# A DiT block's FFN: the first product as a pipeline in a written order, with two units' weight forms made ahead and parked in DRAM

## The chip, the cores and the metric

The kernel runs on one core of one Trainium2 chip. The core has five engines that run side by side, each with its own queue: TensorE (PE, matrix products into PSUM), VectorE (DVE), ScalarE (ACT), GpSimd (POOL) and SyncE (SP, which here issues DMAs). The metric is the device time of one execution in microseconds; the lower the better. All matrix products are made of matmuls with a 128x128 stationary operand and up to 512 moving columns.

## The reference

The program is one block of a diffusion transformer: 1024 tokens of width 1024, in float32, batch 1. What matters here is its second half:

```python
x_new = layer_norm(ALPHA * x + mx[2] * (mix_x @ w_out[l]), ln1_g[l], ln1_b[l])
ffn_x = conv_ffn(modulate(x_new, mx[3], mx[4]), ffn_up[l], ffn_conv_w[l], ffn_conv_b[l], ffn_down[l], rows)
x_new = layer_norm(ALPHA * x_new + mx[5] * ffn_x, ln2_g[l], ln2_b[l])

def conv_ffn(h, w_up, conv_w, conv_b, w_down, grid_rows):
    a, g = jnp.split(h @ w_up, 2, axis=-1)
    a = dwconv3x3(a.reshape(bsz, grid_rows, t // grid_rows, f), conv_w).reshape(bsz, t, f) + conv_b
    return (jax.nn.gelu(a, approximate=False) * g) @ w_down
```

`modulate` is a layer norm over the 1024 features, then a scale and a shift. `ffn_up` is 1024 x 5632 (a half `a` and a gate half `g` of 2816 each), `ffn_down` is 2816 x 1024. The convolution is 3x3 over a grid of 16 x 64 tokens, for each feature by itself.

## The kernel before

Every product is made of three matmuls: each float32 operand is split into a high part (a cast on ACT) and a low part (a subtraction on DVE or POOL), and high x high, high x low and low x high are added in PSUM (`split`, L91; `mm3`, L112).

**w_out** (`out_proj`, L895) takes the tokens in eight row tiles of 128. For each, PE makes 48 matmuls; DVE adds the residual and does the layer norm; after row tiles 2 and 4 the two finished ones are normalised again, modulated and transposed by PE (`modulate2`, L951, `shift2`, L944), which gives the forms "11" and "21" of the FFN's input for the first four row tiles, and copies of them in DRAM (`xr`). Row tiles 4 to 7 stay in SBUF as `ly`.

**FFN, first product.** The 2816 features make 22 units of 128, each with an a column and a g column of `w_up`. A unit's product is done with seven block products instead of eight, Strassen's scheme in Winograd's form: the input X (features x tokens) is cut in four blocks, and so is the unit's weight (a11, a12 of the a column, a21, a22 of the g column). Product k takes one form of the weight and one form of the input (`FORM`, L972): 1 takes a11 and X11, 2 takes a12 and X21, 6 takes S2 and T2, 5 takes S1 and T1, 7 takes a11 - a21 and T3, 3 takes a12 - S2 and X22, 4 takes a22 and T4, with S1 = a21 + a22 and S2 = S1 - a11. One product is 12 matmuls; a unit has 84. The sums of products go through a PSUM bank `x` (tag B, four banks) and a pair `zv` (tag A, two pairs), with copies on ACT and additions on DVE (`after`, L1089).

The weight forms are made in `weight_form` (L983): sums on POOL, the high part on ACT, the low part on POOL, into one of six W tiles. The last part of a unit is the convolution: eight taps on DVE (L1117) on top of a centre tap on ACT (L1096), then the gelu (L1120), the two products with the gate (L1125) and a store of h to DRAM (`hd`, L1126).

`up_begin` (L1023) makes products 1 and 2 of units 0 and 1 and product 1 of units 2 and 3 (72 matmuls) from forms loaded beside w_out (`load_form`), then transposes the last four row tiles (`one`, L1043), makes T2, T1, X22, T3 and T4 from them (`two`, L1053), and runs products 6, 5, 3, 7, 4 of units 0 and 1 together. `ffn_up` (L1135) runs the rest one unit after the other in the order 1, 2, 6, 5, 3, 7, 4, and in units 2 to 9 also makes one column of the modulation (`ada_col`) each. All of this is given to the tile framework, whose scheduler puts each engine's instructions in an order of its own; `high_priority(AHEAD)` lets loads go ahead.

**w_down** (`ffn_down`, L1153) goes over the tokens in two groups of four row tiles, over all 22 units in each; it loads h and w_down again and splits them.

## Time and profile before

| what | us |
|---|---|
| median of three runs | 1412.34 (1410.67 to 1415.03) |
| the profiled execution | 1411.74 |
| its span, first to last instruction | 1409.9 |
| PE busy, share of the span | 1291.0 (92%) |
| DVE busy | 973.6 (69%) |
| ACT busy | 532.7 (38%) |
| POOL busy | 339.6 (24%) |

A busy PE is one that has matmuls in flight. A line such as `L1117 DVE ... x176 | 214.1, 1224 | 5.2 <-ACT` names the line of the kernel, the engine, the operation with its output and inputs, the count, the busy time in us and the mean in ns, and the idle time before it with what ended it. A timeline row starts with the time from the span's start and the duration, both in us. A row of the table by windows gives, for a stretch, each engine's busy time with its number of instructions, then the clock granted to PE (1.00 is full), the share of the DMA engines in use and GB/s.

### The profile page before, as it was taken

To read this page: it belongs to the slowest core of one execution; us is meant where nothing else is said; L and a number is where in the kernel's file an instruction comes from. 1 tells how busy PE (TensorE), PEld (TensorE's weight loads), DVE (VectorE), ACT (ScalarE), POOL (GpSimd) and SP (SyncE) were. 2 spreads that over 40 slices of the span, in tenths; PEclk is the share of its full clock that TensorE was granted. 3 is DMA by queue.
4 is the path that set the end of the run, shared out by engine and by line. 5 is a ranking of instruction groups with operands and counts; after the bars stand their busy time and mean duration, and the time that the engine had idled before them with its cause. 6 is when DMAs were issued, how large, how long until landed. Compare 5 with 4: busy or idle time off the path is not lost.

```text
span 1409.9 us, 17494 instructions
## 1 busy us (share of the span) xinstructions
PE 1291.0 (92%) x6466; PEld 1069.0 (76%) x6466; DVE 973.6 (69%) x1717; ACT 532.7 (38%) x978; POOL 339.6 (24%) x258
## 2 busy tenths in 40 slices
PE   4999999999999999996547999999999959999997
PEld 3888988898888887875435788777878748888885
DVE  7869944869587785888463967666777663339547
ACT  4744434433332413345312344444443423333330
POOL 0000000000000000022808777777777600000000
PEclk9999999999999999998677999999999989999999
DMA  9672310132131541353014422222222128446622
GB/s 336 223 241 72 119 61 30 38 113 75 60 105 31 181 131 66 120 180 134 1 42 158 143 90 75 90 76 75 90 75 90 45 98 290 136 155 215 210 91 89
DMA packets 66661, 163.97 MB, mean 116 GB/s; under 512 B 7808, under 2 KB 10512, under 8 KB 66576
## 3 DMA queue, kind: packets, MB, share of 16 engines
q1 hardware_dynamic: 66576, 162.86, 34.3%
q8 instruction: 50, 0.82, 0.2%
q14 instruction: 35, 0.29, 0.1%
HBM read 140.79 MB, written 22.04 MB: 115 GB/s over the span
## 4 chain that ended last, share of the span: by engine, by line
PE 42%; DVE 6%; POOL 2%; DMA 2%; issue 1%; ACT 1%; DVEq 0%; SPq 0%; POOLq 0%; ACTq 0%
PE psB L1019 5%; PE psB L1021 5%; PE psB L1020 5%; PE psA L1019 4%; PE psA L1020 4%; PE psA L1021 4%; PE psA L114 3%; PE psA L116 3%; PE psA L115 3%; DVE psA L1117 3%; PE psB L114 3%; PE psB L116 3%; PE psB L115 3%; POOL s L997 1%; POOL wf L95 1%
## 5 line engine op out<-in xcount | busy, mean ns | idle before, releaser
L1117 DVE SCALAR_TENSOR_TENSOR psA<-a,par,psA 128x945 f32<-128x945 f32 (+2 forms) x176 | 214.1, 1224 | 5.2 <-ACT psA L1096 1.3
L95 POOL TENSOR_TENSOR wf<-raw,wf 128x512 fp32r<-128x512 f32 x104 | 138.8, 1338 | 115.1 <-ACT wf L94 115.0
L95 POOL TENSOR_TENSOR wf<-r,wf 128x512 fp32r<-128x512 f32 x6 | 8.6, 1464 | 515.3 <-ACT wf L94 515.3
L114 PE MATMUL psA<-xh,wh 128*128 128x512 f32 x320 | 126.7, 396 | 2.3 <-ACT wh L94 1.2
L116 PE MATMUL psA<-xh,wl 128*128 128x512 f32 x320 | 126.0, 394 | 0.1
L115 PE MATMUL psA<-xl,wh 128*128 128x512 f32 x320 | 126.0, 394 | 0.0
L94 ACT CAST wf<-raw 128x512 fp32r<-128x512 f32 x104 | 64.0, 618 | 147.8 <-PE psB L1021 100.5
L95 DVE TENSOR_TENSOR dwl<-r,dwh 128x512 fp32r<-128x512 f32 x80 | 52.4, 690 | 85.5 <-ACT dwh L94 85.1
L1019 PE MATMUL psB<-xk,wf 128*128 128x512 f32 x176 | 73.9, 420 | 36.7 <-DVE r L1122 18.3
L1020 PE MATMUL psB<-x,wf 128*128 128x512 f32 x264 | 104.1, 394 | 0.0
L1095 DVE TENSOR_TENSOR a<-psA,s 128x512 f32<-128x512 f32 x44 | 30.3, 690 | 92.5 <-PE psA L1021 92.5
L94 ACT CAST dwh<-r 128x512 fp32r<-128x512 f32 x80 | 46.6, 620 | 107.8 <-PE psB L116 80.6
L1019 PE MATMUL psA<-x,wf 128*128 128x512 f32 x176 | 72.3, 412 | 8.5 <-ACT wf L94 8.5
L1021 PE MATMUL psB<-xk,wf 128*128 128x512 f32 x176 | 71.8, 408 | 6.5 <-POOL wf L95 6.5
L94 ACT CAST wh<-r 128x512 fp32r<-128x512 f32 x72 | 42.0, 618 | 86.4 <-PE psA L115 59.0
L1019 PEld LDWEIGHTS psB<-xk,wf 128*128 128x128 f32 x176 | 34.8, 198 | 52.3 <-DVE r L1122 26.1
L95 DVE TENSOR_TENSOR wl<-r,wh 128x512 fp32r<-128x512 f32 x72 | 47.5, 688 | 35.9 <-ACT wh L94 22.7
L1019 PE MATMUL psB<-x,wf 128*128 128x512 f32 x176 | 69.1, 392 | 3.0 <-ACT s L1099 3.0
L114 PEld LDWEIGHTS psA<-xh,wh 128*128 128x128 f32 x320 | 60.2, 188 | 14.4 <-ACT wh L94 1.6
L1020 PE MATMUL psA<-x,wf 128*128 128x512 f32 x176 | 69.9, 397 | 0.0
L1021 PE MATMUL psA<-x,wf 128*128 128x512 f32 x176 | 69.6, 395 | 0.2 <-POOL wf L95 0.2
L116 PEld LDWEIGHTS psA<-xh,wl 128*128 128x128 f32 x320 | 60.2, 188 | 12.3 <-DVE wl L95 0.5
(349 smaller groups left out, 3590.3 us busy)
## 6 DMA issues: line engine op xcount, KB each, us to landing
raw<-in_wup SPq DMA_DIRECT2D x44, 512.0 KB, 3.5
r<-in_w_down SPq DMA_DIRECT2D x88, 256.0 KB, 3.2
ada<-in_ada SPq DMA_DIRECT2D x32, 512.0 KB, 3.6
r<-in_win SPq DMA_DIRECT2D x56, 256.0 KB, 2.8
hd<-h SPq DMA_DIRECT2D x22, 512.0 KB, 2.6
hr<-hd SPq DMA_DIRECT2D x44, 256.0 KB, 4.2
adat<-in_ada SPq DMA_DIRECT2D x16, 512.0 KB, 6.9
cada<-in_ada SPq DMA_DIRECT2D x11, 512.0 KB, 5.1
```

The source lines that it names most:

```text
L94: nc.scalar.copy(hi, src)
L95: (on or nc.vector).tensor_tensor(out=lo, in0=src, in1=hi.bitcast(F32), op=ALU.subtract)
L114: mm(out, lh, rh, start=first, stop=False)
L115: mm(out, lh, rl, start=False, stop=False)
L116: mm(out, ll, rh, start=False, stop=last)
L997: pool.tensor_tensor(out=out, in0=x, in1=y, op=op)
L1019: mm(bank, w[:, 0, c], xh, start=start and j == 0, stop=False, skip_group_check=True)
L1020: mm(bank, w[:, 0, c], xl, start=False, stop=False, skip_group_check=True)
L1021: mm(bank, w[:, 1, c], xh, start=False, stop=j == 3, skip_group_check=True)
L1095: nc.vector.tensor_tensor(out=self.a[:, g], in0=z, in1=c, op=ALU.add)
L1117: nc.vector.scalar_tensor_tensor(out=o, in0=a3[:, r0 + di:r1 + di, c0 + dj:c1 + dj], scalar=cw(i, j), in1=o, op0=ALU.mult, op1=ALU.add)
```

## The change

It rewrites the first product of the FFN; w_out's own work and w_down's products stay.

- **Order.** All engines are wrapped (`Engine`), and while `pinned` is set each instruction keeps its place in the program on its engine. The whole of `ffn_up` is pinned. A unit's products come in the order 1, 2, 6, 5, 7, 3, 4, and `step` runs one product, then what follows it, then prepares the weight form five products ahead (`prepare`): the cast on ACT, the subtraction on POOL one step later (`low`). The gelu of a unit comes after product 6 of the next unit, the products with the gate and the store after its product 5.
- **Unit 0 plain.** Unit 0 is done without the seven products, as 96 matmuls (`up_plain`): its first half, on X11 and X21, together with products 1 and 2 of unit 1, takes 72 matmuls ahead of the transposes; its second half follows the transposed tiles three behind.
- **Parking.** The forms of unit 1 (6, 5, 7, 3, 4) and of unit 2 (all seven) are made on POOL beside w_out (`park`: four sums each, a copy and a subtraction for each form) and stored in DRAM by DMAs from POOL's queue; `prepare` loads them back.
- **T forms.** The forms 12 (for the plain unit, in the tiles of T4), 22, T2, T1 and T3 are split on ACT and DVE; T4 on ACT and POOL.
- **Ahead of w_down.** `down_first` loads w_down and h of the first three units during the last unit and splits them on ACT and POOL; w_down begins with these, row tile by row tile in the order 0, 2, 1, 3, banks B for the first two. The last two stores of h go out from POOL's queue.
- The modulation columns are made two at a time in units 5, 7, 9 and 11.

```diff
+        parks = self.park(op, 1, (6, 5, 7, 3, 4)) + self.park(op, 2, (1, 2, 6, 5, 7, 3, 4))
...
+                    if parks and kt in (order[3], order[7]):
+                        parks.pop(0)()
...
+            if t == 7:
+                self.norm2([ys[j] for j in (4, 5, 6)])
...
+    def park(self, op, u, ks):
...
+        def sums():
+            a11, a12, a21, a22 = parts()
+            s = self.Wt((2, 512), F32, nm="ws")
+            r["S1"], r["S2"] = s[:, 0], s[:, 1]
+            pool.tensor_tensor(out=r["S1"], in0=a21, in1=a22, op=ALU.add)
+            pool.tensor_tensor(out=r["S2"], in0=r["S1"], in1=a11, op=ALU.subtract)
+        def sums2():
+            a11, a12, a21, a22 = parts()
+            pool.tensor_tensor(out=a12, in0=a12, in1=r["S2"], op=ALU.subtract)
+            pool.tensor_tensor(out=a21, in0=a11, in1=a21, op=ALU.subtract)
+        def one(k):
+            a11, a12, a21, a22 = parts()
+            src = {1: a11, 2: a12, 3: a12, 4: a22, 5: r.get("S1"), 6: r.get("S2"), 7: a21}[k]
+            w = self.Wt((2, 512), nm="wp")
+            pool.tensor_copy(w[:, 0], src)
+            pool.tensor_tensor(out=w[:, 1], in0=src, in1=w[:, 0].bitcast(F32), op=ALU.subtract)
+            d = self.parked[u, k] = self.dp.tile([P, 2, 512], F32, name=self.name("wd"))
+            nc.gpsimd.dma_start(d, w.bitcast(F32))
...
+        return [raws, sums] + [one_(k) for k in early] + [sums2] + [one_(k) for k in ks if k not in early]
...
+        while self.prepared < min(n + 1, len(self.plan)):
+            u, k = self.plan[self.prepared]
+            self.prepared += 1
+            if (u, k) in self.parked:
+                self.forms[u, k] = self.Wt((2, 512), nm="wf")
+                nc.sync.dma_start(self.forms[u, k].bitcast(F32), self.parked[u, k])
+                continue
...
+            w = self.Wt((2, 512), nm="wf")
+            self.nc.scalar.copy(w[:, 0], src)
+            self.low()
+            self.pending = (w, src)
+            self.forms[u, k] = w
...
+    def low(self):
+        if self.pending:
+            w, src = self.pending
+            self.nc.gpsimd.tensor_tensor(out=w[:, 1], in0=src, in1=w[:, 0].bitcast(F32), op=ALU.subtract)
+            self.pending = None
...
+        b = self.bank("B")
+        self.product(1, b, w11, True)
+        nc.scalar.copy(u1.s[:, 0], b)
+        u0.zv, u1.zv = self.pair(), self.pair()
+        self.up_plain(u0.zv[:, 0], a0, 0)
+        self.product(2, b, w12, False)
+        nc.scalar.copy(u1.a[:, 0], b)
+        ga, gb = self.bank("B"), u1.zv[:, 0]
+        self.up_plain(ga, g0, 0)
+        for j in range(4):
+            nc.sync.dma_start(xa[j // 2][:, j % 2], self.xr[j][:, 0])
+        self.norm2(ys[3:])
...
+        def direct(kt):
+            i, j = kt // 4, kt % 4
+            self.shift2(self.bank("B"), ys, kt, v[j][:, i])
+            self.split(v[j][:, i], *self.form(("12", "22")[i], j))
...
+        order = [0, 4, 1, 5, 2, 6, 3, 7]
+        extra, lag = [], 3
+        for i in range(KT + lag):
+            if i < KT:
+                direct(order[i])
+            if i >= lag:
+                kt = order[i - lag]
+                xh, xl = self.form(("12", "22")[kt // 4], kt % 4)
+                for bank, w in ((u0.zv[:, 1], a0), (gb, g0)):
+                    self.mm3(bank, w[0][:, kt, :], w[1][:, kt, :], xh, xl, i == lag, i == KT + lag - 1)
+            if i == 2:
+                nc.scalar.copy(u0.r[:, 0], ga)
+            if i == 3:
+                self.prepare(1)
+            if i % 2 and i < KT:
+                extra += sums(i // 2)
+            for _ in range(2):
+                if extra:
+                    extra.pop(0)()
+        for f in extra:
+            f()
+        for j in range(4):
+            self.split(xa[j], *self.form("T2", j))
...
+        go(u2, 7)
+        tt(out=u2.r[:, 1], in0=u2.x, in1=u2.r[:, 0], op=ALU.add)
+        self.prepare(self.at + 5)
+        u1.conv()
+        go(u2, 3)
+        tt(out=u2.a[:, 1], in0=u2.v, in1=u2.s[:, 1], op=ALU.add)
+        u2.centre(1, u2.a[:, 1])
+        self.prepare(self.at + 5)
+        go(u1, 4)
+        self.prepare(self.at + 5)
+        u1.gelu()
+        go(u2, 4)
+        self.prepare(self.at + 5)
+        u1.finish((u1.x, u1.r[:, 1]))
+        u2.conv()
+        self.prev = u2
...
+            if k == 2:
+                r[0] = [self.Wt(nm="dwh")]
+                high(r[0][0], flat(0))
+            elif k == 6:
+                r[0].append(self.Wt(nm="dwl"))
+                low(r[0][1], r[0][0], flat(0))
...
+            elif k == 6:
+                nc.scalar.copy(self.s[:, 1], self.x)
+                if b.prev:
+                    b.prev.gelu()
...
+            (nc.sync if self.f < FT - 2 else nc.gpsimd).dma_start(b.hd[self.f], self.h.rearrange("p g t -> p (g t)"))
```

Where the change moves instructions, three places. First POOL's queue from the last instruction ahead of w_out on. Before (`wf` is a weight form, `x` and `xv` belong to the FFN's input, `r` is a raw load):

```order
L293 IOTA masktmp_1084 128x128
L95 TENSOR_TENSOR wf_5647<-r_5648,wf_5647 128x512
L95 TENSOR_TENSOR wf_5652<-r_5653,wf_5652 128x512
L95 TENSOR_TENSOR wf_5657<-r_5658,wf_5657 128x512
L95 TENSOR_TENSOR wf_5662<-r_5663,wf_5662 128x512
L95 TENSOR_TENSOR wf_5667<-r_5668,wf_5667 128x512
L95 TENSOR_TENSOR wf_5672<-r_5673,wf_5672 128x512
L95 TENSOR_TENSOR x_816_5775<-xv_5930,x_814_5773 128x512
```

and with the change (`raw` is a unit's raw weight, `ws` its sums, `wp` a parked form, `wd` its place in DRAM; all calls go through the wrapper's line 57):

```order
L57 TENSOR_TENSOR ws_4901<-raw_4887 128x512
L57 TENSOR_TENSOR ws_4901<-ws_4901,raw_4885 128x512
L57 TENSOR_TENSOR raw_4887<-raw_4885,raw_4887 128x512
L57 TENSOR_TENSOR raw_4885<-raw_4885,ws_4901 128x512
L57 CAST wp_4930<-ws_4901 128x512
L57 CAST wp_4987<-ws_4901 128x512
L57 TENSOR_TENSOR wp_4930<-ws_4901,wp_4930 128x512
L57 TENSOR_TENSOR wp_4987<-ws_4901,wp_4987 128x512
L57 DMA wd_4933<-wp_4930 128x1024
L57 DMA wd_4990<-wp_4987 128x1024
L57 CAST wp_5004<-raw_4887 128x512
```

POOL's first work beside w_out was six subtractions at its end; now 32 operations and twelve DMAs of the parked forms stand there, of which these are the first, and two of the six remain behind them.

Second, ACT's queue where the transposed last row tiles are read. Before (`psA` are the two banks of the pairs that the transposes used in turn; `t2`, `xraw`, `xv` are sums of the input's blocks, `xk` and `x2` their split forms):

```order
L949 ACTIVATE xv855_5930<-psA824_5783,mods_107 128x512
L949 ACTIVATE xv855_5930<-psA825_5784,mods_107 128x512
L949 ACTIVATE xv858_5948<-psA824_5783,mods_107 128x512
L94 CAST x2_814_5773<-xv855_5930 128x512
L94 CAST xk811_5770<-t2856_5931 128x512
L949 ACTIVATE xv858_5948<-psA825_5784,mods_107 128x512
L94 CAST xk812_5771<-xraw854_5929 128x512
```

and with the change (`r881` is the first half of unit 0's gate, out of bank `psB885`):

```order
L57 ACTIVATE xv872_5912<-psB892_6021,mods_107 128x512
L57 CAST xk860_5900<-xv872_5912 128x512
L57 ACTIVATE xv872_5912<-psB893_6029,mods_107 128x512
L57 CAST x2_862_5902<-xv872_5912 128x512
L57 ACTIVATE xv873_5913<-psB894_6039,mods_107 128x512
L57 CAST xk860_5900<-xv873_5913 128x512
L57 COPY r881_5921<-psB885_5975 128x512
L57 ACTIVATE xv873_5913<-psB895_6049,mods_107 128x512
```

The tile that comes out of a transpose is now cast at once, without a sum ahead of it, and the transposes go round four B banks, the fourth of which (`psB895`) is the one that the copy of `psB885` frees.

Third, the end of POOL's queue, in the FFN's last unit. Before:

```order
L95 TENSOR_TENSOR wf1243_9036<-raw1231_8959,wf1243_9036 128x512
L95 TENSOR_TENSOR wf1245_9064<-raw1232_8960,wf1245_9064 128x512
L95 TENSOR_TENSOR wf1246_9081<-raw1232_8960,wf1246_9081 128x512
L1285 UNCONDITIONAL_BRANCH
L1285 ISA
```

and with the change (`dw` and `dr` belong to w_down's weights, `dh` to its h, `hd` is h in DRAM):

```order
L57 TENSOR_TENSOR wf1271_9064<-raw1233_8761,wf1271_9064 128x512
L57 TENSOR_TENSOR dwl1275_9098<-dr1264_9038,dwh1273_9081 128x1024
L57 DMA hd20_95<-h1274_9096 128x1024
L57 TENSOR_TENSOR dhw1278_9120<-dr1267_9041,dhw1278_9120 128x512
L57 TENSOR_TENSOR dwv1279_9123<-dr1266_9040,dwv1279_9123 128x1024
L57 TENSOR_TENSOR dhr1281_9127<-dr1267_9041,dhr1280_9126 128x512
L57 TENSOR_TENSOR dwl1283_9167<-dr1265_9039,dwh1282_9143 128x1024
L57 TENSOR_TENSOR dhw1284_9181<-dr1268_9042,dhw1284_9181 128x512
L57 DMA hd21_96<-h1285_9184 128x1024
```

The low parts of w_down's first three units and the stores of the last two units' h have moved here.

More of the change, by code (lines that the diff above doesn't have):

```diff
@@ L44, in strided, with __init__, __getattr__, call @@
     return bass.AP(t.tensor, t.offset + off, [list(t.ap[0])] + [list(d) for d in dims])
+class Engine:
+    def __init__(self, b, engine):
+        self.b, self.engine = b, engine
+    def __getattr__(self, name):
+        f = getattr(self.engine, name)
+        def call(*args, **kw):
+            ins = f(*args, **kw)
+            return self.b.tc.keep_in_program_order(ins) if self.b.pinned else ins
+        return call
+class Engines:
+    def __init__(self, b, nc):
+        for e in ("tensor", "vector", "scalar", "gpsimd", "sync"):
+            setattr(self, e, Engine(b, getattr(nc, e)))
 class Builder:
@@ L50, in __init__ @@
     def __init__(self, tc, a, out):
-        self.tc, self.nc, self.a, self.out = tc, tc.nc, a, out
+        self.tc, self.a, self.out = tc, a, out
+        self.pinned = False
+        self.nc = Engines(self, tc.nc)
         self.n = 0
@@ L981, in load_form, with load_raws @@
         return w
[L983 to L992 removed]
+    def load_raws(self, u):
+        ra, rg = self.S((2, 512), nm="raw"), self.S((2, 512), nm="raw")
+        for r, f in ((ra, u), (rg, FT + u)):
+            self.nc.sync.dma_start(r.rearrange("p j (k f) -> p (j k) f", f=P), self.a["wup"][f])
+        self.raws[u] = dict(a=ra, g=rg)
@@ L1014, in product @@
+            self.forms[u, k] = w
+        if self.prepared == len(self.plan):
+            self.low()
+    def low(self):
[3 more added lines that the diff above has]
+            self.pending = None
+    def product(self, k, bank, w, start):
+        mm = self.nc.tensor.matmul
         for j in range(4):
@@ new lines, in product, with up_plain @@
+            mm(bank, w[:, 0, c], xh, start=start and j == 0, stop=False, skip_group_check=True)
+            mm(bank, w[:, 0, c], xl, start=False, stop=False, skip_group_check=True)
+            mm(bank, w[:, 1, c], xh, start=False, stop=j == 3, skip_group_check=True)
+    def up_plain(self, bank, w, g):
+        for kt in range(KT):
+            xh, xl = self.form(("11", "21", "12", "22")[2 * g + kt // 4], kt % 4)
+            self.mm3(bank, w[0][:, kt, :], w[1][:, kt, :], xh, xl, kt == 0, kt == KT - 1)
@@ L1128, in units @@
-    def units(self, us, ks):
-        for k in ks:
-            ws = [self.weight_form(u.f, k) for u in us]
-            self.product(k, [(u.open(k), w, k in (1, 2, 5)) for u, w in zip(us, ws)])
-            for u in us:
-                u.after(k)
-    def ffn_up(self):
-        nc = self.nc
-        bufs = dict(raw=4, a=2, s=2, r=2, h=3)
-        self.ut = lambda kind: self.up.tile([P, 2, 512], F32, tag=kind, bufs=bufs[kind], name=self.name(kind))
-        silc = self.up.tile([P, D], F32, tag="row", bufs=2, name="silc5")
-        nc.sync.dma_start(silc, self.silc[0:1].broadcast_to([P, D]))
-        for f in range(2, FT):
-            if f < 10:
-                t = self.up.tile([P, D], F32, tag="row", bufs=2, name=self.name("ada"))
-                nc.sync.dma_start(t, self.a["ada"][38 + f])
-                self.ada_col(38 + f, silc, self.mods[:, 38 + f:39 + f], [t])
-            elif f == 10:
-                self.gate5 = self.gate_line(5)
-            if f < 4:
-                self.units([self.begun[f - 2]], (2, 6, 5, 3, 7, 4))
-            else:
-                self.units([self.Unit(self, f)], (1, 2, 6, 5, 3, 7, 4))
+                tt(out=self.a[:, 1], in0=self.zv[:, 1], in1=self.s[:, 1], op=ALU.add)
@@ L1157, in ffn_down @@
             LAST = 3 if g == 0 else 7
-            banks = [[self.bank("A" if t < 2 else "B") for _ in range(2)] for t in range(4)]
-            late = []
+            order = (0, 2, 1, 3) if g == 0 else range(4)
+            banks = {t: [self.bank(("B" if t < 2 else "A") if g == 0 else "A" if t < 2 else "B") for _ in range(2)] for t in order}
+            late, early = [], []
             def work(t, c, f, hh, wh, wl):
@@ L1226, in ffn_down, with down_load @@
                     self.finish(ys[t], t, lng, lnb, st)
+    def down_load(self, dn, g, f, i):
+        nc, hh = self.nc, None
+        if i is not False:
+            if i % 2 == 0:
+                self.big = self.kp.tile([P, 4, D], F32R, tag="kq", bufs=2, name=self.name("dwk"))
+            wh, wl = self.big[:, 2 * (i % 2), :], self.big[:, 2 * (i % 2) + 1, :]
+            hh = self.Wt((2, 512), nm="dhw")
+        else:
+            wh = dn.tile([P, D], F32R, tag="dwh", bufs=4, name=self.name("dwh"))
+            wl = dn.tile([P, D], F32R, tag="dwl", bufs=4, name=self.name("dwl"))
+            hh = dn.tile([P, 2, 512], F32R, tag="dh", bufs=4, name=self.name("dh"))
+        hh = hh[:, 0, :], hh[:, 1, :]
+        for c in range(2):
+            c = slice(c * 512, (c + 1) * 512)
+            self.load_split(self.a["w_down"][f * P:(f + 1) * P, c], wh[:, c], wl[:, c])
+        with self.tc.high_priority(self.AHEAD):
+            h = dn.tile([P, 512], F32, tag="hr", bufs=6, name=self.name("hr"))
+            nc.sync.dma_start(h, self.hd[f][:, g * 512:(g + 1) * 512])
+            self.split(h, *hh)
+        return wh, wl, hh
     def load_xnew(self, dn, t):
```

377 lines of the change are left out of this document (242 added, 135 removed).

## The prediction

> **What bounds the kernel now.** I read the page's slices first, then busy times by stage, then the timelines inside the stages that stand out.
>
> ```profile
> PE   4999999999999999996547999999999959999997
> PEclk9999999999999999998677999999999989999999
> ```
>
> TensorE (PE) is full everywhere but in two dips, slices 19 to 22 and 33; its clock falls there too. The stages, by windows:
>
> ```profile
> core 0: us, PE busy (x) PEld busy (x) DVE busy (x) ACT busy (x) POOL busy (x), PEclk, DMA share, GB/s
> 552.50:609.10 56.60, 56.60 (x255) 45.38 (x254) 45.94 (x145) 20.87 (x62) 0.00 (x0) 1.00 0.25 84
> 635.30:652.30 17.00, 17.00 (x80) 14.10 (x79) 12.71 (x48) 5.69 (x10) 0.00 (x0) 1.00 0.52 189
> 652.30:809.30 157.00, 97.02 (x369) 72.93 (x367) 101.33 (x107) 55.62 (x91) 96.81 (x68) 0.78 0.25 86
> 809.30:1138.00 328.70, 328.70 (x1418) 263.47 (x1419) 228.46 (x221) 138.15 (x220) 233.07 (x177) 1.00 0.23 77
> 1138.00:1158.30 20.30, 4.85 (x21) 3.34 (x20) 12.30 (x12) 2.42 (x3) 0.00 (x0) 0.74 0.23 68
> 1158.30:1401.00 242.70, 242.25 (x1056) 198.72 (x1056) 134.40 (x245) 75.58 (x137) 0.00 (x0) 0.99 0.53 177
> 1401.00:1409.90 8.90, 0.00 (x0) 0.00 (x0) 5.62 (x13) 0.20 (x1) 0.00 (x0) 0.66 0.15 59
> ```
>
> The w_out product (to 635.3) and the FFN from 809.3 to 1138 leave PE no idle time. From 652.3 to 809.3 PE works 97 of 157 us at a clock of 0.78, and before w_down 20.3 us pass. These two are what the change can win. What fills the first, from PE's timeline and the chain of waits:
>
> ```profile
> 676.96 0.80 PE L1019 MATMUL psB<-xk,wf 128*128 128x512 f32 x1 [14.05 <-ACT s L1087]
> ```
> ```profile
> 708.38 16.02 DVE psA L1117 x15
> 736.11 6.53 DMA raw<-in_wup
> ```
>
> PE waits 14 us for the forms of the last four row tiles, then 16 us for the convolutions of two units run together, then for a weight load that stood in SP's queue behind a store.
>
> **The change, part by part.** *Steady stretch.* A unit begins here every 19.50 us, 84 matmuls at 0.232 (chain of waits):
>
> ```profile
> 828.61 0.67 PE psB L1019 x2
> 848.11 0.68 PE psB L1019 x2
> ```
> ```profile
> L1117 DVE SCALAR_TENSOR_TENSOR psA<-a,par,psA 128x945 f32<-128x945 f32 (+2 forms) x176 | 214.1, 1224 | 5.2 <-ACT psA L1096 1.3
> ```
> ```profile
> L95 POOL TENSOR_TENSOR wf<-raw,wf 128x512 fp32r<-128x512 f32 x96 | 128.4, 1341 | 106.7 <-ACT wf L94 106.7
> ```
>
> The new order keeps 84 matmuls and gives each engine's instructions in program order. I walked one unit through the queues. Per unit DVE has eight taps (9.8 us) and some 4 us of additions; the ada columns now come two at a time in four units, two more operations of 1024 columns, each like a tap: 16.3 us. POOL has eleven operations at 1.34, 14.7 us, and a form is ready four products before its use. Pinning adds one wait that others stand behind: ACT's gelu waits for the previous unit's convolution, and behind it stand a cast and the copy of product 5. That convolution starts when product 3 ends, at 16.7, and ends near 28.5, 9 us into the next unit; the copy is wanted when product 3 starts, at 14. So 19.5 stays; POOL would bind only above 19.5/11 = 1.77 us an operation.
>
> *Start of the FFN.* PE first gets 72 matmuls, as many as before, then the transposes of the last four row tiles:
>
> ```profile
> 651.63 1.03 PE L948 MATMUL psA<-ident,ly 128*128 128x128 f32 x8
> ```
> ```profile
> 655.04 0.62 ACT L94 CAST xk<-t 128x512 fp32r<-128x512 f32 x1
> 655.56 0.78 ACT L949 ACTIVATE xv<-psA,mods 128x512 f32<-128x512 f32 x1
> 656.23 0.61 ACT L94 CAST xk<-xraw 128x512 fp32r<-128x512 f32 x1
> ```
> ```profile
> 660.33 0.68 DVE L95 TENSOR_TENSOR x<-xraw,xk 128x512 fp32r<-128x512 f32 x1
> 660.93 0.68 DVE L1048 TENSOR_TENSOR xraw<-xv,xraw 128x512 f32<-128x512 f32 x1
> ```
>
> From 651.6 on these now run beside the second half of unit 0's plain products, which need no sums, only the tile split once; before, every next product needed T2. The splits that POOL made here (forms 22 and T3) go to DVE, and POOL, which holds DVE up (below), is nearly idle. A tile costs ACT 0.67 + 0.52 = 1.19 us, DVE 0.60 an operation. PE's fourth transpose needs the bank that ACT empties only after three tiles and a copy, 4.9 us in; three transposes fill 1.6, so PE idles 3.3, and I add 2 for a lowered clock. DVE's 20 operations (eight splits, twelve sums) end some 14 us in, with POOL's four subtractions between them 17, and T2's four splits at 19.4; its first use is at 24. ACT casts T1 after unit 0's end (18.7) and T3 after two copies, so T3 is done at 26.5, wanted at 31. To the end of unit 2: 32 transposes 4.1, the remaining 48 + 60 + 84 = 192 matmuls 44.5, one matmul with the identity (no row: 0.23 like a product's to four transposes' 0.52; I take 0.5, it is f32 as they are), 5.3 for the fill: 54.4, so 706.0. Parked forms come by DMA five products (14 us) ahead, and a load lands in 3.5:
>
> ```profile
> raw<-in_wup SPq DMA_DIRECT2D x44, 512.0 KB, 3.5
> ```
>
> Then DVE is late, since three convolutions come in 45 us. Unit 0's runs from 26.5 to 36.3. Unit 1's stands in DVE's queue behind the addition after unit 2's product 7, which ends at 44.9: it ends at 55, its gelu at 59, and unit 3's second product needs that pair of banks at 56: 2.7 us. Unit 2's convolution ends at 70, and its gelu stands ahead of the copy that unit 3's product 3 waits for: 2.5. Bounds: 0, if the fill is longer and hides it, to 10, one chain of eight taps. I take 5.2, by the walk: 711.2. With 19 units at 19.5 the FFN ends at 1081.7, against 1138. Before, 328.7/19.5 = 16.9 units were left at 809.3, so 5.1 were done; now 5.1 are done at 711.2 + 2.1 x 19.5 = 753.
>
> *w_out.* Here POOL had nothing before 622. Parking gives it 32 operations (20 with two inputs, twelve casts), twelve DMA issues and four loads on SP. A row for its casts does not exist: between ACT's 0.62 and POOL's 1.34. An issue on POOL: SP's 0.33 to 1.34; that is 4 to 16 us of POOL, off the path. What counts is what POOL does to DVE:
>
> ```profile
> 622.22 1.07 DVE L136 TENSOR_TENSOR nwt<-vet,rst 128x1 f32<-128x1 f32 x1
> 625.82 2.29 DVE L866 SCALAR_TENSOR_TENSOR ly<-ly,rst,ln_b 128x1024 f32<-128x1024 f32 x1
> 632.23 0.16 DVE L136 TENSOR_TENSOR nwt<-vet,rst 128x1 f32<-128x1 f32 x1
> 632.81 1.28 DVE L866 SCALAR_TENSOR_TENSOR ly<-ly,rst,ln_b 128x1024 f32<-128x1024 f32 x1
> ```
> ```profile
> 621.95 8.57 POOL L95 TENSOR_TENSOR wf<-r,wf 128x512 fp32r<-128x512 f32 x6 [515.27 <-ACT wf L94]
> ```
>
> With POOL at work a DVE operation that reads two SBUF tiles takes 1.0 us longer (1.07 for 0.16, 2.29 for 1.28). And PE has no slack for it: the normalised tile is done by ACT at 583.64, its transpose ran at 583.82, at a fixed place in PE's queue, which the change leaves where it was; behind it stand all of w_out's later matmuls. A second norm step stands 25 us later in the same way.
>
> ```profile
> 582.40 1.24 ACT L942 ACTIVATE ly<-ly,nmt,rst 128x1024 f32<-128x1024 f32 x1 [1.45 <-DVE nmt L941]
> ```
> ```profile
> 583.82 0.49 PE L948 MATMUL psB<-ident,ly 128*128 128x128 f32 x3
> ```
> ```profile
> L149 DVE BATCH_NORM_STATS2 bnst<-ly 128x6 f32<-128x512 f32 x22 | 14.1, 678 | 0.0
> L931 DVE SCALAR_TENSOR_TENSOR ly<-ly,psA 128x512 f32<-128x512 f32 x14 | 9.0, 672 | 0.0
> ```
>
> DVE is busy 45.9 of 56.6 us there; in the 10.7 it idles some eight of POOL's operations fit. The statistics and the PSUM additions, 23 us and some small ones, read one SBUF tile, and L931 at 0.67 shows no delay; the other 0.6 of DVE's busy time reads two. 24 x 0.6 x 1.0 = 14 us lost. Bounds: 0, if POOL fits into what is idle, to 32 x 1.34 = 43 (a lower clock after each of two stalls is in it). I take 14, since the two rows with POOL beside them are of this very stage. By the Trainium skill (SBUF — State Buffer, Who interferes with whom) the two engines share a port as a lock, and the later one blocks for the other's whole instruction. The trace agrees in kind, at 1.0 us where whole operations take 1.34; by the rule's letter the 14 would be 24 x 0.6 x 1.34 = 19.
>
> The new wait on SP: the raw weights of unit 2 wait until POOL is done with unit 1's, and the load of x for row tile 2 and three stores stand behind them.
>
> ```profile
> 564.55 0.33 SPq L922 DMA_DIRECT2D ly<-in_x  x1
> ```
>
> POOL can start near 552; twelve operations and two issues later it is 572. With 3.5 to land, x is there at 576; the product that it is added to ends 34 matmuls, 8 us, ahead of the transpose at 583.82, so near 576: free, or as late as POOL is, which the 43 covers.
>
> *w_down.* The chain of waits in the second dip:
>
> ```profile
> 1139.56 1.21 DVE psA L1117
> 1150.17 1.03 ACT h L1120
> 1153.00 4.53 DMA hr<-hd
> 1158.28 0.80 PE psA L114
> 1161.62 0.23 PE psA L115
> ```
>
> Convolution, gelu, product, store and reload, then eight matmuls at half speed. Now the weights and h of the first three tiles are made during the last unit by ACT and POOL, and PE goes on with 72 matmuls (16 us), longer than the last unit's 10.4 us of convolution, gelu and product. Only row tile 1's second bank waits for that product: 1.5. Without this cover the 20.3 come back. w_down takes 242.7 less 2.0 of slow start, the end 8.9.
>
> **Sum.** 1081.7 + 14 + 1.5 + 240.7 + 8.9 = 1346.8 against 1409.9, less 63. The profiled run's time was 1411.74, 1.84 over its span, and the median 1412.34 is 0.6 above that: 1346.8 + 2.4 = 1349.
>
> **Rivals.**
> 1. *Parking is free*: DVE's delay fits in gaps. For it: DVE idles 10.7 us of the 56.6. Against: 0.18 us of slack. 1349 - 14 = 1335. Chance 0.17.
> 2. *Every POOL operation blocks DVE whole*, 43 us instead of 14: 1378. For it: DVE is 0.8 full, so delays add up. Against: one-tile operations between. Chance 0.13. The lock of the Trainium skill (SBUF — State Buffer, Who interferes with whom) is this mechanism.
> 3. *The fill fails*: DVE late with T2 or T3 and a gap of one convolution pair, 16 us, with slow clock 22: 1371. For it: DVE is the fullest engine there. Chance 0.12.
> 4. *w_down's start is not covered*, the change not doing there what it says (the lows of w_down and the last two stores stand in POOL's one queue): plus 19, 1368. Chance 0.06.
> 5. *Slower*: in the pinned order every unit waits for POOL's lows. From 1.77 us an operation it decides; at 2.15 a unit takes 23.7, plus 4.2 x 19 = 80: 1429. For it, POOL beside a busy DVE:
>
> ```profile
> 671.33 1.71 POOL L997 TENSOR_TENSOR s<-raw 128x512 f32<-128x512 f32 x1
> ```
>
> Against: 1.34 in the steady stretch, beside the same DVE work per unit. Chance 0.04.
>
> **How the numbers follow.** Forecast 0.48, own range 1340 to 1359 (w_out 5 to 24). The range 1332 to 1376 takes in rivals 1, 3, 4 and part of 2 and leaves out 5. A measurement tells 0.3%, 4.2 us, from no change: faster 0.94, same 0.01, slower 0.05.
>
> **What would show it.** DVE's small operations near 1.1 us in w_out beside POOL, and PE idle before the transposes of both norm steps there; one PE gap of 3 to 5 us after the first 72 matmuls; units 19.5 apart; no PE gap over 2 us before w_down. Wrong: a steady unit above 20, w_out unchanged or more than 30 us longer, or a gap over 10 us in the first three units.

## The result, and the profile after

| | before | after |
|---|---|---|
| median of four runs, us | 1412.7 (1410.7 to 1415.0) | 1368.7 (1364.4 to 1371.5) |
| ratio, 95% interval | | 0.969 (0.966 to 0.972) |
| profiled execution: time, span | 1411.74, 1409.9 | 1371.46, 1369.7 |

The change makes the kernel 3.1% faster: 44 us, where the prediction had 63. In the profile of the change every line is that of the wrapper (L57), so groups are told by their tiles. The slices of the page after:

```profile
PE   4999999999999999949998999999999999999997
POOL 0000000000000000560027766677777740000000
PEclk9999999999999999969999999999999999999999
```

Before w_down (slice 33 before) no dip is left, and that at the start of the FFN has shrunk to one 8. A new dip stands in slice 17, inside w_out, just where POOL has got work. The stages, by windows: w_out, the first 72 matmuls of the FFN, the rest up to the end of unit 2, unit 3, units 4 to 11, units 12 to 21, w_down, end.

```profile
core 0: us, PE busy (x) PEld busy (x) DVE busy (x) ACT busy (x) POOL busy (x), PEclk, DMA share, GB/s
540.90:660.98 120.08, 99.16 (x417) 77.01 (x417) 101.90 (x228) 41.33 (x125) 41.61 (x46) 0.90 0.46 165
660.98:677.35 16.37, 16.37 (x73) 13.47 (x72) 11.47 (x40) 6.53 (x10) 0.00 (x0) 1.00 0.46 154
677.35:731.02 53.67, 50.00 (x228) 39.50 (x226) 44.79 (x52) 31.40 (x51) 19.16 (x14) 1.00 0.50 178
731.02:757.46 26.44, 21.27 (x86) 16.78 (x84) 19.83 (x20) 10.78 (x17) 16.82 (x14) 0.94 0.33 112
757.46:922.84 165.38, 156.65 (x674) 128.06 (x672) 122.49 (x129) 66.15 (x104) 113.46 (x90) 0.98 0.33 116
922.84:1113.39 190.55, 190.55 (x842) 157.68 (x841) 130.86 (x131) 84.44 (x131) 137.70 (x107) 1.00 0.24 82
1113.39:1360.10 246.71, 242.36 (x1057) 198.75 (x1055) 139.83 (x248) 73.77 (x133) 4.22 (x4) 0.99 0.51 170
1360.10:1369.70 9.60, 0.16 (x1) 0.00 (x0) 5.62 (x13) 0.20 (x1) 0.00 (x0) 0.65 0.15 55
```

Ten units in 190.55 us are 19.05 a unit, so the steady pipeline runs at PE's pace. What is lost lies in four places. The first and largest, from PE's and ACT's timelines in w_out (in brackets the idle time before, and what ended it):

```profile
600.35 0.48 PE L57 MATMUL psB<-ident,ly 128*128 128x128 f32 x1 [14.52 <-ACT ly L57]
607.20 0.90 PE L57 MATMUL psB<-ident,ly 128*128 128x128 f32 x3 [2.96 <-ACT ly L57]
```
```profile
599.05 1.24 ACT L57 ACTIVATE ly<-ly,nmt,rst 128x1024 f32<-128x1024 f32 x1 [15.10 <-DVE nmt L57]
```

PE waits 14.5 us for the first transpose of the norm step, and the norm waits for DVE. What DVE and POOL did in that time:

```profile
589.03 0.69 DVE L57 TENSOR_TENSOR ml<-O,mh 128x128 fp32r<-128x128 f32 x1
589.64 5.47 DVE L57 TENSOR_TENSOR ml<-sgo,mh 128x128 fp32r<-128x128 f32 x2
595.03 3.14 DVE L57 TENSOR_TENSOR ml<-O,mh 128x128 fp32r<-128x128 f32 x1
598.10 0.15 DVE L57 SCALAR_TENSOR_TENSOR rst<-nwt,rst 128x1 f32<-128x1 f32 x1
```
```profile
588.90 0.67 POOL L57 CAST wp<-raw 128x512 fp32r<-128x512 f32 x1
...
590.11 1.27 POOL L57 TENSOR_TENSOR wp<-raw,wp 128x512 fp32r<-128x512 f32 x1
591.34 1.26 POOL L57 TENSOR_TENSOR raw<-raw,raw 128x512 f32<-128x512 f32 x1
592.54 0.57 POOL L57 DMA_DIRECT2D wd<-wp  x1
593.13 1.27 POOL L57 TENSOR_TENSOR raw<-raw,ws 128x512 f32<-128x512 f32 x1
594.34 1.23 POOL L57 CAST wp<-ws 128x512 fp32r<-128x512 f32 x2
```

The last three of these tile splits, 0.28 us each when POOL is idle, take 8.6 us here, while POOL makes unit 2's forms. The chain's small operation `rst`, 0.15 long, stands behind them. Summed over DVE's timeline from 553 to 610 us (each operation less the shortest of its form), 19 operations are held up by 22.5 us in all, beside 32 POOL operations of 33.5 us. This sum is "DVE held up" in the table below.

The other three places: unit 3 (26.4 us for 19.04); four units of 4 to 11, those with two modulation columns, which take 21.5 to 23.1; and a stall in w_down, 20 us after its start. Rows of PE's timeline for each:

```profile
737.29 4.57 PE L57 MATMUL psA<-x,wf 128*128 128x512 f32 x12 [3.39 <-ACT h L57]
751.87 3.03 PE L57 MATMUL psA<-x,wf 128*128 128x512 f32 x12 [1.78 <-ACT psA L57]
792.44 4.60 PE L57 MATMUL psA<-x,wf 128*128 128x512 f32 x12 [2.18 <-ACT psA L57]
834.61 3.01 PE L57 MATMUL psA<-x,wf 128*128 128x512 f32 x12 [2.18 <-ACT psA L57]
1133.83 0.50 PE L57 MATMUL psB<-dwh,dh 128*128 128x512 f32 x1 [2.94 <-ACT dh L57]
```

### The profile page after: what moved, and what is told of

Its sections match the earlier page's. It is cut to its first block, busy times and chain, and to the rows that moved or that the text cites. A ratio compares the mean times of both kernels' runs of the same rounds, so it can differ in the third digit from the quotient of the medians.

```text
span 1369.7 us, 17583 instructions
## 1 busy us (share of the span) xinstructions
PE 1284.1 (94%) x6480; PEld 1074.6 (78%) x6480; DVE 977.1 (71%) x1712; ACT 528.3 (39%) x966; POOL 334.1 (24%) x279
## 5 line engine op out<-in xcount | busy, mean ns | idle before, releaser
L57 DVE SCALAR_TENSOR_TENSOR psA<-a,par,psA 128x945 f32<-128x945 f32 (+2 forms) x176 | 215.9, 1227 | 21.6 <-ACT psA L57 16.2
L57 PE MATMUL psA<-x,wf 128*128 128x512 f32 x708 | 175.7, 398 | 15.2 <-ACT psA L57 11.8
L57 PE MATMUL psB<-xk,wf 128*128 128x512 f32 x672 | 176.8, 390 | 1.0 <-ACT s L57 1.0
L57 PEld LDWEIGHTS psA<-x,wf 128*128 128x128 f32 x708 | 135.5, 192 | 46.6 <-ACT psA L57 14.3
L57 PEld LDWEIGHTS psB<-xk,wf 128*128 128x128 f32 x672 | 126.2, 188 | 27.9 <-ACT s L57 1.4
L57 POOL TENSOR_TENSOR wf<-raw,wf 128x512 fp32r<-128x512 f32 x95 | 124.5, 1322 | 62.8 <-ACT wf L57 62.7
L57 PE MATMUL psA<-xh,wh 128*128 128x512 f32 x320 | 127.4, 398 | 2.1 <-ACT wh L57 1.2
L57 PE MATMUL psA<-xh,wl 128*128 128x512 f32 x320 | 126.6, 396 | 0.1
L57 PE MATMUL psA<-xl,wh 128*128 128x512 f32 x320 | 126.6, 396 | 0.0
L57 POOL TENSOR_TENSOR ws<-raw 128x512 f32<-128x512 f32 x2 | 2.6, 1282 | 460.3 <-DMA raw<-in_wup 460.3
L57 DVE TENSOR_TENSOR dwl<-r,dwh 128x512 fp32r<-128x512 f32 x74 | 48.4, 688 | 81.1 <-ACT dwh L57 81.0
L57 PE MATMUL psB<-x,wf 128*128 128x512 f32 x384 | 104.7, 389 | 0.0
L57 PE MATMUL psB<-dwh,dh 128*128 128x512 f32 x296 | 98.5, 394 | 2.9 <-ACT dh L57 2.9
L57 PE MATMUL psA<-dwh,dh 128*128 128x512 f32 x296 | 97.3, 390 | 0.7 <-DVE fy L57 0.7
L57 PEld LDWEIGHTS psB<-x,wf 128*128 128x128 f32 x384 | 72.1, 188 | 15.4 <-issue 0.2
L57 ACT CAST dwh<-r 128x512 fp32r<-128x512 f32 x74 | 43.0, 619 | 102.8 <-PE psA L57 67.0
L57 ACT CAST wh<-r 128x512 fp32r<-128x512 f32 x76 | 44.6, 618 | 92.1 <-PE psA L57 64.5
L57 DVE TENSOR_TENSOR a<-psA,s 128x512 f32<-128x512 f32 x39 | 26.9, 691 | 72.1 <-PE psA L57 72.1
L57 DVE TENSOR_TENSOR wl<-r,wh 128x512 fp32r<-128x512 f32 x76 | 49.9, 685 | 36.1 <-ACT wh L57 22.8
L57 ACT CAST wf<-raw 128x512 fp32r<-128x512 f32 x95 | 58.5, 616 | 42.3 <-PE psA L57 27.4
L57 PEld LDWEIGHTS psA<-xh,wh 128*128 128x128 f32 x320 | 60.5, 189 | 14.2 <-ACT wh L57 1.6
L57 PEld LDWEIGHTS psA<-xh,wl 128*128 128x128 f32 x320 | 60.6, 189 | 12.5 <-DVE wl L57 0.5
```

The costliest lines, as they stand in the source:

```text
L57: ins = f(*args, **kw)
```

## The experiments

Eleven kernels ran, each in three rounds beside the kernel before. Nine differ from the change in one place (one in two); two put together what the others showed. Length of w_out here is from its first matmul to the FFN's first product: 96.2 us before, 120.1 after. A kernel whose ratio overlaps the change's 0.966 to 0.972 (five of the nine) is not clear of the change by its time alone; what is said of gains of 2 to 5 us rests on the profile.

| what differs from the change | time, us | ratio to before, 95% | w_out, us | DVE held up, us |
|---|---|---|---|---|
| nothing (the change) | 1368.7 | 0.966 to 0.972 | 120.1 | 22.5 |
| parking without arithmetic | 1343.9 | 0.949 to 0.953 | 96.7 | 0 |
| parking's loads from POOL's queue | 1365.8 | 0.965 to 0.968 | 117.4 | 19.7 |
| parking's POOL operations halved in width | 1366.1 | 0.965 to 0.968 | 115.8 | 22.3 |
| parking's casts on ACT | 1364.6 | 0.965 to 0.968 | 117.2 | 19.4 |
| parking on DVE and ACT | 1349.0 | 0.952 to 0.956 | 103.1 | 0 |

### Is it POOL's arithmetic, or SP's queue?

The prediction named both: POOL's hold on DVE, and a load on SP that waits for POOL. First the arithmetic was left out:

```diff
-            pool.tensor_tensor(out=r["S1"], in0=a21, in1=a22, op=ALU.add)
-            pool.tensor_tensor(out=r["S2"], in0=r["S1"], in1=a11, op=ALU.subtract)
...
-            pool.tensor_tensor(out=a12, in0=a12, in1=r["S2"], op=ALU.subtract)
-            pool.tensor_tensor(out=a21, in0=a11, in1=a21, op=ALU.subtract)
...
-            pool.tensor_copy(w[:, 0], src)
-            pool.tensor_tensor(out=w[:, 1], in0=src, in1=w[:, 0].bitcast(F32), op=ALU.subtract)
...
-            nc.gpsimd.dma_start(d, w.bitcast(F32))
+            nc.gpsimd.dma_start(d, r[k % 2])
```

> The parking keeps its loads, its twelve stores and their places, but leaves out all 32 arithmetic operations on POOL: raw weights are stored as forms, so units 1 and 2 of the FFN compute with wrong weights. Theory 1 (POOL's operations hold up DVE's operations with two SBUF inputs): the 14.5 and 3.0 us of idle PE before the transposes go, and the half clock after them; w_out ends 22 us earlier, near 638, and the time is about 1347. Theory 2 (what hurts is SP's queue, where loads stand behind a load that waits for the parking): the waits of SP stay, since the stores out of the raw tiles release it no sooner; w_out ends after 650 and the time stays above 1360.

Measured: 1343.9, w_out 96.7 us, the length before the change. The same splits, now with no POOL operation beside them, and the transpose that waited 2.96 us, by DVE's and PE's timelines:

```profile
557.26 0.49 DVE L57 TENSOR_TENSOR ml<-O,mh 128x128 fp32r<-128x128 f32 x2 [5.41 <-PE psA L57]
557.67 0.49 DVE L57 TENSOR_TENSOR ml<-sco,mh 128x128 fp32r<-128x128 f32 x2
```
```profile
583.90 0.55 PE L57 MATMUL psB<-ident,ly 128*128 128x128 f32 x3 [0.68 <-ACT ly L57]
```

Two splits take 0.49 us; in the change the same two took 2.51. But without arithmetic SP's wait was shorter too (the load of x went out at 564.7 and not at 571.6), so that wait was taken away by itself, with POOL's work kept:

```diff
-                nc.sync.dma_start(r[i].rearrange(...), self.a["wup"][f])
+                nc.gpsimd.dma_start(r[i].rearrange(...), self.a["wup"][f])
```

> The parking's four loads of raw weights are issued from POOL's queue; nothing on SP waits for the parking any more, POOL's 32 operations stay. Theory 1 (POOL's operations hold up DVE): w_out stays 116 to 122 us long (96.2 before the change, 120.1 after), with PE idle over 8 us at the transposes, and the time stays within 1362 to 1374. Theory 2 (SP's queue): w_out falls below 108 and the time to 1350 to 1357.

Measured: 1365.8, w_out 117.4. Nothing of the parking is left on SP, and the stall at the transposes is what it was:

```profile
599.97 0.48 PE L57 MATMUL psB<-ident,ly 128*128 128x128 f32 x1 [14.45 <-ACT ly L57]
```

So SP's wait does not cost PE these 14 us, and the arithmetic does. What SP's wait did in the change was to set when unit 2's forms are made: POOL idled 9.5 us for a load and then ran from 584.5 on, into the norm step. With the loads on its own queue it ran from 574.4 to 597.7 and met the norm step all the same; one DVE operation of 1.27 us took 6.33 there.

### What sets the size: the operation or the work?

```diff
+        def tt(out, x, y, op):
+            for c in (slice(0, 256), slice(256, 512)):
+                pool.tensor_tensor(out=out[:, c], in0=x[:, c], in1=y[:, c], op=op)
...
-            pool.tensor_tensor(out=a21, in0=a11, in1=a21, op=ALU.subtract)
+            tt(a21, a11, a21, ALU.subtract)
...
-            pool.tensor_copy(w[:, 0], src)
-            pool.tensor_tensor(out=w[:, 1], in0=src, in1=w[:, 0].bitcast(F32), op=ALU.subtract)
+            for c in (slice(0, 256), slice(256, 512)):
+                pool.tensor_copy(w[:, 0, c], src[:, c])
+            tt(w[:, 1], src, w[:, 0].bitcast(F32), ALU.subtract)
```

> Each of the parking's 32 POOL operations is cut into two of half the width (64 of about 0.65 us), the work as a whole is the same or 2 to 4 us more. If a DVE operation waits for the end of the POOL operation that is running, each wait is half as long: the 22 us of delays of DVE in w_out fall to 11 to 14, w_out from 120 to 106 to 112 us, the time to 1355 to 1361. If DVE is held up for as long as POOL has work in a row, whatever its pieces, w_out stays at 117 to 123 and the time at 1364 to 1372.

Measured: 1366.1, in the band of the second theory; w_out, 115.8, is nearer to it too. The profile shows why. DVE's timeline in a stretch of splits:

```profile
557.36 1.16 DVE L57 TENSOR_TENSOR ml<-O,mh 128x128 fp32r<-128x128 f32 x2 [5.41 <-PE psA L57]
558.44 1.58 DVE L57 TENSOR_TENSOR ml<-sco,mh 128x128 fp32r<-128x128 f32 x2
559.94 0.83 DVE L57 TENSOR_TENSOR ml<-O,mh 128x128 fp32r<-128x128 f32 x1
```

One wait is halved, as the first theory says: 0.83 - 0.28 = 0.55 us instead of 1.1. But now 35 operations wait instead of 19, and the sum is the same, 22.3 us: in this stretch DVE gets one operation through between two of POOL's, so with more of these it waits more often. Neither theory was whole, and cutting the work smaller won nothing clear of noise. It also made the work larger: the 64 halves took 43.5 us of POOL where the 32 took 33.5 (2 to 4 us more were expected). So the run does not tell whether halves of the same total would have held DVE up less. Nor does any run tell why some DVE operations wait for one POOL operation and some for several (here up to 2.4 us for 0.15).

The casts (12 of the 32, one input each) went to ACT:

```diff
-            pool.tensor_copy(w[:, 0], src)
+            nc.scalar.copy(w[:, 0], src)
```

> The parking's twelve casts go to ACT, POOL keeps the 20 operations with two inputs. If every POOL operation that reads SBUF holds DVE up, casts too (DVE's operations beside them end with them), POOL's 37 us of work fall to 26 and w_out's loss of 23.8 us to 14 to 18: 1359 to 1364. If casts with one input cost nothing, the time stays at 1366 to 1371. If the holes that POOL gets by waiting for ACT let DVE through each time, the loss falls below 10 and the time below 1356.

Measured: 1364.6, between the bands of the first two cases and nearer to the first; DVE is held up 19.4 us beside 26.8 us of POOL instead of 22.5 beside 33.5. By these sums casts cost something, but less than their share. That a cast holds DVE up the trace of the change shows directly (above: the split at 589.03, 0.69 for 0.28, beside the cast at 588.90); how much each kind costs this run does not settle, since without the casts POOL's work also lies elsewhere.

### Where else could the parking go?

```diff
-        nc, pool = self.nc, self.nc.gpsimd
+        nc, pool = self.nc, self.nc.vector
...
-            pool.tensor_copy(w[:, 0], src)
+            nc.scalar.copy(w[:, 0], src)
```

> The parking's 20 sums and subtractions go from POOL to DVE, its twelve casts to ACT; the output stays the reference's. Theory 1 (the lock between POOL and DVE): DVE gets 20 x 0.6 = 12 us of work, but nothing waits for a POOL operation of 1.3 us any more: w_out ends 10 to 20 us earlier, the time is 1350 to 1360. If DVE has no room for work at all there (12 us of work delay the norm steps as much as POOL did), w_out ends where it did and the time stays at 1365 to 1372.

Measured: 1349.0, 20 us less than the change, with the same work. DVE, the fullest engine after PE there, does the 20 operations itself in 12 us and loses less than by waiting for POOL to do them. PE's idle time at the transposes is 2.2 us:

```profile
588.20 0.66 PE L57 MATMUL psB<-ident,ly 128*128 128x128 f32 x4 [2.21 <-ACT ly L57]
```

Of the 6.9 us that w_out is still longer than before, another 2.8 is PE waiting for a row tile whose load of x went out on SP behind eight stores.

### The modulation columns

```diff
-                if k == 6 and f in (5, 7, 9, 11):
-                    for i in range(2): ... self.ada_col(j, ...)
+                if k == 6 and f in range(4, 12):
+                    self.ada_col(36 + f, ...)
```

> The eight modulation columns are made one each in units 4 to 11 instead of two each in units 5, 7, 9 and 11. Theory: two columns (4.7 us of DVE) between the end of the previous unit's convolution and the addition of product 5 make the copy late that product 3 waits for; one column (2.3 us) fits. The four stalls (units of 23.1, 21.5, 23.0, 21.6 instead of 19.04, 13.1 us in all) go, the time is 1355 to 1357. Rival: it is DVE's total work that decides, not the place; then eight units lose half as much each and the time stays at 1368.

Measured: 1366.2 (ratio 0.966, 0.963 to 0.968). All eight units take 20.17 us, so in the profile 9.0 us are lost instead of 13.1. The rival was nearer. But total work is not it either, as the next run shows, with the column behind product 5's operations (`if k == 5`):

> One modulation column each in units 4 to 11, but behind the three DVE operations that follow product 5, not ahead of them. Theory (place): the copy that product 3 waits for no longer stands behind the column; DVE idles there until product 7 ends, so all eight units fall from 20.17 to 19.04 and the time is 1356 to 1358. Rival (total of DVE's work, POOL's hold on it in it): the column now makes product 7's addition late, product 4 waits for it, and a unit stays at 20 or above: 1365 or more.

Measured: 1357.3 (ratio 0.961, 0.960 to 0.963), every unit from 4 to 21 at 19.04 on average. The place decides. DVE's timeline, one column ahead of the addition `a` of product 5 (first fence) and behind it (second):

```profile
769.18 2.32 DVE L57 CUSTOM_DVE_ANT_0 ada<-ada,silc 128x1024 f32<-128x1024 f32 x1
771.43 0.08 DVE L57 DVE_READ_ACCUMULATOR2_ANT adaacc<- 128x1 f32 x1
771.54 1.13 DVE L57 TENSOR_TENSOR mods<-adaacc,par 128x1 f32<-128x1 f32 x1
772.60 0.68 DVE L57 TENSOR_TENSOR a<-psA,s 128x512 f32<-128x512 f32 x1
```
```profile
785.54 0.69 DVE L57 TENSOR_TENSOR a<-psA,s 128x512 f32<-128x512 f32 x1 [1.99 <-PE psA L57]
787.34 1.22 DVE L57 CUSTOM_DVE_ANT_0 ada<-ada,silc 128x1024 f32<-128x1024 f32 x1
788.61 1.12 DVE L57 TENSOR_TENSOR mods<-adaacc,par 128x1 f32<-128x1 f32 x1
789.65 0.68 DVE L57 TENSOR_TENSOR r<-psB,r 128x512 f32<-128x512 f32 x1
```

Ahead of it, the column takes 3.4 us, 2.1 of them POOL's hold (2.32 for 1.22, 1.13 for 0.16), and ACT's copy for product 3 waits for the addition behind it. That price was the same for one column and for two (2.27 + 1.13 and 1.21 + 0.16 in the change), which is why halving the columns did not halve the stall. Behind it, the column fills time in which DVE waits for product 7.

### Unit 1's convolution, and the load of h

```diff
+        u1.conv()
         go(u2, 7)
         tt(out=u2.r[:, 1], in0=u2.x, in1=u2.r[:, 0], op=ALU.add)
         self.prepare(self.at + 5)
-        u1.conv()
```

and in `down_load` h ahead of the weights.

> Two edits at places far apart. Unit 1's convolution is put ahead of unit 2's product 7 and its addition: DVE idles 4.8 us there now; it starts 5 us earlier, and unit 3 (26.4 us, stalls of 3.4 and 1.8 and a half clock) falls to 19.5 to 20.5: 6 to 7 us. And in w_down h is loaded ahead of the weights: the stall of 3.1 us 20 us after w_down's start, with its half clock, goes: 4.8 us. Together 1357 to 1359. Rivals: the stall moves to unit 2's product 4, which then waits for the addition behind the convolution (gain under 3); in w_down the weights of the fourth slice are themselves late, and nothing is won.

Measured: 1363.8 (ratio 0.965, 0.963 to 0.968), above the 1357 to 1359 expected. The convolution starts without the 4.8 us of idle DVE before it; unit 3 takes 20.8 instead of 26.4, and unit 2's product 4 now waits 0.5: about 5 us, a little under the 6 to 7 expected. The load of h won nothing. SP's timeline in the change shows what h stands behind (start, and how long the three took to issue):

```profile
1093.04 36.66 SPq L57 DMA_DIRECT2D r<-in_w_down  x3
1129.75 0.42 SPq L57 DMA_DIRECT2D hr<-hd  x1
```

The third of these loads waits until 1129.3 for a buffer: two of the four hold the split h of the second slice, which PE reads until then. The scheduler put h behind it in either order of the program.

### The work ahead of w_down undone

```diff
-            if f == last:
-                ahead = self.down_first()
...
-                if f == last:
-                    ahead(k)
...
-                if g == 0 and f < 3:
-                    wh, wl, hh = self.ready[f]
-                else:
+                if True:
```

> Only the work ahead of w_down is undone: the first three slices of w_down and h are loaded and split as before the change, behind the last unit, with the order of w_down's products as in the change otherwise. Forecast's step: without the cover the 20.3 us between the last product and w_down come back, less the two stalls that the change has there now (1.1, and 3.1 with its half clock): the time rises by 13 to 16, to 1381 to 1385. If the cover is worth nothing, 1368.

Measured: 1379.1 (ratio 0.976, 0.974 to 0.977), 10.3 more, under the 13 to 16 expected. PE idles 13 us where the change idles 0.7, and starts at half clock:

```profile
1113.40:1126.50 13.10, 0.39 (x2) 0.00 (x0) 11.71 (x13) 3.63 (x7) 0.53 (x1) 0.66 0.00 0
1126.50:1369.20 242.70, 242.14 (x1056) 199.03 (x1056) 133.45 (x245) 73.70 (x135) 0.00 (x0) 0.99 0.53 177
```

So the cover works, but without it only 13 us of idle PE come back, not 20.3: in the new order the last two stores go out from POOL's queue, so SP's loads of h stand behind none of them, and the chain of waits goes from the last gelu straight to ACT's casts. And the change gives 4.6 us back in the stall of h, which this kernel has not.

### Put together

The parking on DVE and ACT, the earlier convolution, the columns behind product 5, and h of the fourth slice loaded from POOL's queue:

> Put together: the parking on DVE and ACT, unit 1's convolution earlier, the modulation columns one each behind product 5, and the load of h for the fourth slice of w_down from POOL's queue instead of SP's. Single gains read so far: 19.7, 5.0 (in the trace), and expected 10 and 4 to 5. If they add up: 1368.7 - 39 = 1329 to 1332. If the h load is not what makes w_down's start late, 1334; if the columns' new place wins nothing, 1340.

Measured: 1334.7 (ratio 0.945, 0.943 to 0.946): the second case of the expectation. The single gains without h (19.7, 5.0 and 11.4) would make 1332.6; the measured time is 2 us above that, and h won nothing. Its load came early enough, but its cast stood on ACT behind the cast of weights that the same blocked load brings. So the buffers were freed, w_out's stores moved, and the load of h went back to SP's queue:

```diff
-            self.nc.sync.dma_start(self.xr[kt % 4][:, kt // 4, c], v)
+            self.nc.gpsimd.dma_start(self.xr[kt % 4][:, kt // 4, c], v)
...
-                y = [self.wp.tile([P, 512], F32R, tag="R", ...) for _ in range(2)]
+                y = self.kp.tile([P, 4, D], F32R, tag="kq", ...)
```

> As the version that was put together, but with two changes of the transfers: the stores of the modulated input go out from POOL's queue (in w_out a load of x stood behind them on SP and PE waited 3.2 us for its row tile, with a half clock after it), and in w_down's start the split h of the second slice lies in a tile that the input forms have left, so that all four weight buffers are free and no load of SP waits for w_down itself. From 1334.7: 3 to 5 us in w_out, 4 to 5 in w_down: 1325 to 1328. If the load of x is late for another reason, 1330.

Measured: 1327.8, ratio 0.939 (0.938 to 0.941): nearly twice the change's gain over the kernel before. Its windows, for w_out, unit 3, units 4 to 21 and w_down:

```profile
538.27:638.97 100.70, 95.28 (x416) 74.37 (x417) 85.83 (x234) 47.28 (x136) 17.70 (x30) 1.00 0.55 197
711.50:732.30 20.80, 19.33 (x85) 15.69 (x84) 16.57 (x16) 8.68 (x14) 16.05 (x14) 1.00 0.43 140
732.30:1075.43 343.13, 343.13 (x1515) 283.77 (x1513) 252.94 (x259) 150.93 (x235) 250.57 (x196) 1.00 0.31 111
1075.43:1317.20 241.77, 240.46 (x1057) 197.66 (x1055) 139.37 (x248) 73.12 (x133) 4.20 (x4) 1.00 0.51 168
```

What is left: w_out is 4.5 us longer than before, PE idles 5.4 us between it and unit 3, and unit 3 is 1.8 over a steady unit.

## Why the prediction was right, and where it was not

The direction, most of the mechanisms and the wide range of 1332 to 1376 held; the likeliest time, 1349, was 20 us short, and the measured one lies 10 us outside the forecast's own range of 1340 to 1359. By its terms, in the profiled execution (span 1346.8 predicted, 1369.7 measured):

| term | predicted, us | measured, us |
|---|---|---|
| up to w_out's first matmul | 0 | +1.8 |
| w_out, longer by | 14 | 23.9 |
| FFN's start to the end of unit 2 | 70.7 | 70.0 |
| units 3 to 21, late convolutions in it | 375.7 | 382.4 |
| w_down with the gap before it | 242.2 | 246.7 |
| end | 8.9 | 9.6 |

One sum of the working is off by one (711.2 + 2.1 x 19.5 is 752, not 753); no term hangs on it.

- **w_out: the mechanism right, the size wrong.** "24 x 0.6 x 1.0 = 14 us lost" is the term that failed most. The figures beside its 0.6 are of two stretches: the 23 us of one-input work are counted over 545 to 635, the 45.9 of busy DVE over 552.5 to 609.1. In the shorter stretch 22.6 of the 45.9 read at most one SBUF tile, so the share there is 0.5 and the term 12, further off still. Both factors were too small: 19 operations waited, not 24 x 0.6 = 14, and 1.2 us on average, not 1.0. The two rows with POOL beside them showed one wait of 1.0 each. In a run of POOL operations one DVE operation waited for up to five (5.27 us), the sum was 22.5, and PE idled 19.3 us more than before and ran at half clock until 612, 4.6 us more. The half clock was only in the bound, not in the 14. By the rule of the Trainium skill (SBUF — State Buffer, Who interferes with whom) a DVE instruction with two SBUF inputs contends with a GpSimd instruction that reads SBUF, and one with a single SBUF input, outside DVE's two-port modes, does not. The trace agrees: an addition that reads PSUM takes its 0.67 beside the casts at 599.07 (last section). The prediction's estimate by this rule, 19, was nearer than 14; but it has one wait for one instruction, and the waits of 3.14 and 5.27 us here go past that. By "the second norm step in the same way" two stalls were due; only the first came, since POOL was done by 606.7.
- **SP's new wait** was put near 572 and judged free: it ended at 571.6, and taking it away did not shorten the stall.
- **The fill** was right in sum, not in kind: "PE idles 3.3" for a bank did not happen (16 transposes ran in 2.1 us), and four waits of 0.2 to 1.3 us fell on later matmuls instead.
- **Late convolutions**: both stalls stood where the walk put them (unit 3's second product and its product 3), at 3.4 and 1.8 us for 2.7 and 2.5. That sum was right, 5.2; but with the half clock after the first, which the walk left out, unit 3 lost 7.4.
- **The steady unit** "stays 19.5": it was 19.04. Before, a few matmuls of each unit started up to 0.34 us apart instead of 0.227, which makes up the 0.46; with the change hardly any do. But four units were above 20, the mark set for being wrong. The step at fault is "16.3 us" of DVE in 19.5: a sum over a unit, where the place counted. The walk had the convolution's end 9 us into the unit and the copy wanted at 14; it left out that the columns and the addition stand between them, and that POOL adds 2.1 us there. This cost 13.1 us. The table shows only 6.7 for units 3 to 21, by luck: at the steady pace 19 units are 8.7 us shorter than forecast, and that hid part of the stalls.
- **w_down**: the gap is gone as said (0.7 us are left of it). Not foreseen was the shared buffer that holds SP's queue: 2.9 us and 1.7 of half clock.

Of the rivals, the first (parking is free), the third (the fill), the fourth (no cover) and the fifth (POOL sets the unit) are out; that the measured time is the fourth's 1368 is chance, since the gap before w_down is gone. The truth lay between the forecast and the second rival, whose 43 us would need DVE to wait through all of POOL's work: w_out grew by 23.9.

## What to carry to other kernels

An idle engine is not free if it shares something with a full one: ask not how long each of its operations is, but how much of the full engine's work must take turns with it, and whether that work stands ahead of a fixed place in PE's queue. A sum of busy time per unit shows that work fits, not that it fits where it is put; for each moved operation name what stands behind it in its queue. And a buffer lent to a look-ahead can stop the queue that feeds the next stage.
